# Up projection of an encoder layer: the transposes of six column groups moved from TensorE to DMA, on 16-bit planes that ScalarE splits and joins

## The chip, the cores and the metric

The kernel runs on one core of a Trainium2 chip. The metric is the device time of one launch in microseconds. Three runs of the kernel before gave 1339.71 to 1340.78 us, with a median of 1339.76 us.

## The reference

One layer of a transformer trunk on 256 tokens of width 2048, in float32: two kinds of attention, gates, an output projection, and then the part that is touched here, an MLP with a squared ReLU.

```python
h = rms_norm(x, norm_mlp_pre[l])                                             # 256 x 2048
u = jnp.square(jax.nn.relu(jnp.einsum('bsd,df->bsf', h, w_up[l])))           # 256 x 8192
x = x + rms_norm(jnp.einsum('bsf,fd->bsd', u, w_down[l]), norm_mlp_post[l])  # 256 x 2048
```

The up projection leaves `u` with tokens on the 128 partitions. The down projection sums over the 8192 columns of `u`, so it needs `u` transposed: columns on the partitions, tokens along the row.

## The kernel before

Each float32 operand of a product is split into a high part (`h`, rounded to TensorE's float32r) and a low part (`l`, what the rounding left). A product is then three matmuls: high by high, high by low, low by high. For each weight block ScalarE makes the high part (`CAST u_4h<-u_4r`) and VectorE subtracts to get the low one (`TENSOR_TENSOR u_4l<-u_4r,u_4h`). Every low part therefore waits for a cast of ScalarE.

The up projection runs in eight groups `g` of 1024 columns. A group is eight steps, each with one weight block of 256 by 1024 numbers (`u_0r` to `u_7r`, 1 MB, issued on SyncE's queue). Where a step is marked "seven" in `UPS`, the product is done with seven multiplications instead of eight, on sums of quarters of the weight block: `u_0t`, `u_3t`, `u_5t` are these sums, made by VectorE, `eh` their high parts (ScalarE), `el` their low ones (VectorE). Two tiles of sums stand after one another, the second made from the first, so VectorE and ScalarE take turns on them. The list `UPS` sets the order of the blocks within a group: 1, 2, 0, 4, 3, 6, 5, 7. Weights are prepared two steps ahead of their use (`Weights.next`), in a pool `wp` of three buffers each for the raw block, its high and its low part. A shared pool `pages` of 27 buffers holds everything else.

At the end of a group ScalarE and VectorE take the eight accumulators out of PSUM (`combine` and `u_piece`), scale and rectify them, and leave two tiles `z[0]`, `z[1]` of 128 tokens by 1024 columns. While the next group runs, `up_each(n)`, called ahead of each step `n` of it, treats these tiles: at steps 1 and 2 `u_T` transposes 512 columns each on TensorE (eight matmuls with the identity into two PSUM banks) and ScalarE squares them on the way out; at steps 3 and 5 `u_sets` splits the transposed `u` again into high and low parts (`ah`, `al`, for one of the two halves with the sums `sm`, made by VectorE). GpSimd's queue stores these parts to memory (`keeph`, `keepl`), and the down projection loads them again much later. The last group's results and those of the one before it are needed at once, and their transposes stand in other places (group 7 and the first steps of the down projection).

A scheduler orders the instructions of each engine: it plays the program with costs of its own and puts first what it finds ready first. Semaphores for all dependences are added after that. Each engine works through its row in that order; an instruction that waits holds up all that stand behind it on its engine, and a DMA issued from ScalarE's queue stands in ScalarE's row.

Of the kernel before, what the change touches and what calls it, by code (L numbers as in the profile page):

```python
# [10 lines left out]

F32 = mybir.dt.float32
F32R = mybir.dt.float32r
AF = mybir.ActivationFunctionType
ALU = mybir.AluOpType
AX = mybir.AxisListType

P = 128
D = 2048
T = 256  # L20
KD = D // P
DFF = 4 * D
# [28 lines left out]
def encoder_layer(ctx: ExitStack, tc: tile.TileContext, a, out):  # L51
    nc = tc.nc
# [12 lines left out]
    def page(shape, dt, name):  # L65
        return pages.tile(shape, dt, tag="pg", name=name)
# [4 lines left out]
    def t2k(name, dt=F32):  # L71
        return tmp.tile([P, 2, T], dt, tag="t2k", name=name, bufs=7)
# [6 lines left out]
    def small(w, name):  # L79
        return tiny.tile([P, w], F32, tag=f"s{w}", name=name)  # L80
# [37 lines left out]
    def split(raw, name, pieces=2, after=(), then=None):  # L118
# [3 lines left out]
        _, nk, cw = (P, len(raw), 512) if listed else raw.shape  # L122
        hi = wp.tile([P, nk, cw], F32R, tag="hi", name=f"{name}_h")
        lo = wp.tile([P, nk, cw], F32R, tag="lo", name=f"{name}_l")
        prev = front if then else ()
# [170 lines left out]

    hT = [page([P, 2, 512], F32R, f"hT{i}") for i in range(8)]

    def x_part(k):
# [3 lines left out]
        g = g_pre[:, k : k + 1]  # L303
        i = nc.scalar.activation(d[:, :T], src, AF.Copy, scale=g).ins
        j = nc.vector.scalar_tensor_tensor(  # L305
# [30 lines left out]
    def x_squares(i):  # L336
        for t in range(2):
            j = junk512("jx0").rearrange("p a b -> p (a b)")
            nc.scalar.activation(
                j, xp[i][:, t], AF.Square, accum_out=ssx[:, t * 4 + i : t * 4 + i + 1]  # L340
            )
# [10 lines left out]
    def head_constants():  # L352
# [5 lines left out]
        le = small(2, "le")  # L358
        nc.scalar.activation(le, ls, AF.Exp)
        nc.vector.scalar_tensor_tensor(  # L360
# [55 lines left out]
    def parts(dst, at, src):  # L416
        hi, lo = dst
        nc.scalar.copy(hi[at], src)
        nc.vector.tensor_sub(lo[at], src, hi[at].bitcast(F32))
# [34 lines left out]
    def v_evac(dst):  # L454
        hi, lo = dst

        def evac(t, ps):
            r = rx[:, t : t + 1]
            nc.scalar.activation(hi[:, t], ps, AF.Copy, scale=r)
            nc.vector.scalar_tensor_tensor(  # L460
# [5 lines left out]
    def p_transposed(p, name):  # L466

        pt = bank(f"{name}_pt")
        for kt in range(2):
            for t in range(2):  # L470
# [4 lines left out]
                )  # L475
        r = [t2k(f"{name}_pT{i}", F32R) for i in range(2)]
        parts(r, slice(None), pt.rearrange("p (k q) -> p k q", k=2))
        return r

    def diff_head(h, qT, kT, v, hl, sc):  # L480
        p = t2k(f"dp{h}")
        for t in range(2):
# [19 lines left out]
            for c in range(2):  # L502
                nc.scalar.activation(
                    e[:, c],
                    s[:, c * T : (c + 1) * T],
                    AF.Exp,
                    bias=nbs[:, c : c + 1],
# [27 lines left out]
        for t in range(2):  # L535
            nc.scalar.activation(
                on[:, t], o[:, t * T : (t + 1) * T], AF.Square, accum_out=ss[:, t : t + 1]
            )
# [5 lines left out]
        for eb in range(2):  # L544
            for t in range(2):
# [4 lines left out]
                )  # L550
        ot = page([P, 2, 512], F32R, f"oaT{h}")
        for eb in range(2):
# [8 lines left out]
    def na_head(h, qT, kT, v, hl):  # L561
# [47 lines left out]
        if h % 2 == 0:  # L609
            oT["nt", h // 2] = page([P, 2, 512], F32R, f"onT{h}")  # L610
        ot = oT["nt", h // 2][:, h % 2]
# [283 lines left out]
    for h in range(2):  # L895
        gate = []
        for br, gc, src, o in (("a", GA, a["w_branch_a"], "a"), ("b", GB, a["w_branch_b"], "n")):
            z = [page([P, 2, 512], F32, f"g{br}{h}{t}") for t in range(2)]
# [183 lines left out]
    def first_up(n):  # L1082
        for t, c in {2: [(1, 1), (0, 2)], 3: [(1, 2), (0, 3)], 4: [(1, 3)]}.get(n, ()):
            residual_parts(t, c)
        if n == 5:
            for t in range(2):
                mlp_squares(t)
                mlp_scale(t)
            for i in range(4):
                kd = dram.tile([P, 1024], F32, name=f"keepx{i}", tag=f"keepx{i}")  # L1090
                nc.gpsimd.dma_start(kd, x2[i])
                kept["x", i] = kd
# [67 lines left out]
    def u_T(cg, z):  # L1160
# [12 lines left out]
            )  # L1173
        return u

    def u_sets(cg, u):

        got = act_sets(cg, u)
        if NG - 4 <= cg < NG - 2:
            sets[0, cg] = got  # L1180
# [34 lines left out]
                uw.ask(wd[:, :, cg, j, g * 1024 : (g + 1) * 1024], f"d{g}{cg}{j}", seven, page)  # L1215
    uz = None
    us = {}
    for g in range(DFF // 1024):
        z = Late(lambda g=g: [page([P, 2, 512], F32, f"u{g}{t}") for t in range(2)])

        def up_each(n, g=g, uz=uz):
            if not g:
                first_up(n)
                if n == 7:
                    for i in (0, 3, 5):
                        f = page([P, 2, T], F32, f"h2f{i}")
                        for k in range(2):
                            d = hT2[i][:, k].bitcast(F32)
                            nc.vector.tensor_add(f[:, k], d[:, :T], d[:, T:])
                        h2sum[i] = sums_of(f[:, 0], f[:, 1], f"h2s{i}")  # L1230
                return
            cg = g * 2 - 3 + n
            if n in (1, 2):
                us[cg] = u_T(cg, uz)
            steps = (3, 5) if g < DFF // 1024 - 1 else (1, 2)
            if n in steps:
                cg = g * 2 - 2 + steps.index(n)
                u_sets(cg, us[cg])

        wide_group(  # L1240
            f"u{g}",
            ups(g),
            uw,
            h2stat7,
            h2stat8,
            (1, 2, 3, 7),
            z,
            partial(u_piece, z=z),
            each=up_each,
            turn=None if g else turn_rows,  # L1250
            after={} if g else {2: scaled[0]},
        )
        uz = z
# [102 lines left out]
    for g in range(2):  # L1356
        pr = Products(f"p{g}", (1, 2, 3, 7))
        pr.in_order = True
        for bi, b in enumerate(blocks[g]):
            end = bi == len(blocks[g]) - 1  # L1360
            for n, (cg, j, seven) in enumerate(down_steps(g, bi)):
# [42 lines left out]
                for which in range(4):  # L1404
# [4 lines left out]
                    if last:  # L1409
                        bank_, t, half = PLAIN[which]  # L1410
# [65 lines left out]
```

## Time and profile before

| | before |
|---|---|
| median of three runs | 1339.76 us |
| the profiled execution | 1339.83 us |
| its span, first to last instruction | 1338.1 us |
| mean granted TensorE clock | 0.997 |
| TensorE matmul busy | 1326.8 us (99%) |
| VectorE busy | 1097.9 us (82%) |
| ScalarE busy | 739.4 us (55%) |
| transposes `uT` on TensorE | 128, of which 32 are those of group 7 and of the start of the down projection |

The profiled execution is 0.07 us above the median. The 1.7 us between its time and its span are start and end. In rows of the time line the columns are start, duration, engine, line, operation, output and inputs with shapes, count, and in brackets how long the engine had been idle before it and on what. In the chain, the columns are start, duration, engine, tile, line, count. The busy time of an engine is a sum over its instructions, and weight loads of TensorE (PEld) lie beside its matmuls.

### The profile page before, as it was taken

How to read it: one execution, taken by the hardware profiler on the slowest of the kernel's cores; microseconds unless marked ns; L12 is line 12 of the kernel's file. 1: busy time of each engine (PE TensorE's matmuls, PEld its weight loads, DVE VectorE, ACT ScalarE, POOL GpSimd, SP SyncE). 2: the span in 40 equal slices, each digit the busy share in tenths (PEclk: the TensorE clock that was granted, in tenths of full speed). 3: DMA queues.
4: the chain of work that ended last, by engine and by line, in shares of the span. 5: the costliest groups of instructions: out<-in, count | busy, mean ns of one | idle time of the engine just before them, and what ended most of it. 6: DMA issues, size and time to landing. Idle time of an engine off the chain costs nothing.

```text
span 1338.1 us, 16265 instructions
## 1 busy us (share of the span) xinstructions
PE 1326.8 (99%) x6297; PEld 1112.1 (83%) x6297; DVE 1097.9 (82%) x1279; ACT 739.4 (55%) x866; POOL 38.5 (3%) x71
## 2 busy tenths in 40 slices
PE   9999999999999999999999999999999999999997
PEld 8888888888888888888888888888888888888885
DVE  7978866667777888885688999999978888898886
ACT  6655554544545555555476666666555554555542
POOL 0000000000000000000100000000000000000000
PEclk9999999999999999999999999999999999999998
DMA  9874655564565656567657777877797998798995
GB/s 343 279 219 162 197 168 176 184 186 157 189 220 172 207 187 213 184 233 256 228 184 274 243 251 270 302 238 245 251 362 287 402 375 314 265 376 331 353 356 202
DMA packets 113981, 335.85 MB, mean 251 GB/s; under 512 B 16752, under 2 KB 17008, under 8 KB 113904
## 3 DMA queue, kind: packets, MB, share of 16 engines
q1 hardware_dynamic: 94512, 266.13, 57.9%
q10 hardware_dynamic: 12672, 43.00, 8.4%
q0 software_dynamic: 6720, 25.69, 5.0%
q8 instruction: 49, 0.80, 0.2%
q14 instruction: 28, 0.23, 0.0%
HBM read 307.01 MB, written 29.61 MB: 252 GB/s over the span
## 4 chain that ended last, share of the span: by engine, by line
PE 96%; DMA 1%; DVE 1%; ACT 0%; SPq 0%; issue 0%; DVEq 0%; POOLq 0%; POOL 0%; ACTq 0%
PE u L740 25%; PE p L740 24%; PE ga L740 6%; PE gb L740 6%; PE ba L740 3%; PE bb L740 3%; PE y L740 3%; PE qn_p L221 2%; PE kn_p L221 2%; PE ka_p L221 2%; PE qn_p L223 1%; PE kn_p L223 1%; PE qa_p L221 1%; PE vn_p L264 1%; PE va_p L265 1%; PE vn_p L265 1%
## 5 line engine op out<-in xcount | busy, mean ns | idle before, releaser
L221 PE MATMUL qn_p<-hT,qn_h 128*128 128x512 f32 x128 | 45.8, 399 | 0.0
L221 PE MATMUL ka_p<-hT,ka_h 128*128 128x512 f32 x128 | 45.1, 397 | 0.2 <-DVE rope_s L291 0.2
L221 PE MATMUL kn_p<-hT,kn_h 128*128 128x512 f32 x128 | 45.3, 397 | 0.0
L221 PE MATMUL qa_p<-hT,qa_h 128*128 128x512 f32 x128 | 43.9, 402 | 0.4 <-DVE hT L305 0.4
L740 PE MATMUL u<-u_2h,h2T 128*128 128x512 f32 x128 | 44.0, 396 | 0.0
L740 PE MATMUL u<-u_1h,h2T 128*128 128x512 f32 x128 | 43.4, 390 | 0.0
L740 PE MATMUL u<-u_4h,h2T 128*128 128x512 f32 x128 | 43.2, 391 | 0.0
L740 PE MATMUL u<-u_7h,h2T 128*128 128x512 f32 x128 | 41.0, 389 | 0.0
L740 PE MATMUL u<-u_6h,h2T 128*128 128x512 f32 x128 | 41.0, 389 | 0.0
L223 PE MATMUL qn_p<-hT,qn_l 128*128 128x256 f32 x128 | 35.9, 281 | 0.0
L223 PE MATMUL kn_p<-hT,kn_l 128*128 128x256 f32 x128 | 35.7, 280 | 0.0
L223 PE MATMUL ka_p<-hT,ka_l 128*128 128x256 f32 x128 | 35.1, 280 | 0.0
L223 PE MATMUL qa_p<-hT,qa_l 128*128 128x256 f32 x128 | 32.4, 281 | 0.0
L145 DVE TENSOR_TENSOR y_l<-y_w,y_h 128x1024 fp32r<-128x1024 f32 x16 | 19.0, 1221 | 11.9 <-ACT y_h L137 11.9
L221 PEld LDWEIGHTS ka_p<-hT,ka_h 128*128 128x128 f32 x128 | 23.8, 188 | 5.7 <-DVE rope_s L291 0.7
L221 PEld LDWEIGHTS qn_p<-hT,qn_h 128*128 128x128 f32 x128 | 24.1, 188 | 5.2
L145 DVE TENSOR_TENSOR kn_l<-kn_w,kn_h 128x1024 fp32r<-128x1024 f32 x16 | 19.0, 1220 | 11.3 <-ACT kn_h L137 11.2
L221 PEld LDWEIGHTS kn_p<-hT,kn_h 128*128 128x128 f32 x128 | 23.9, 188 | 5.2
L221 PEld LDWEIGHTS qa_p<-hT,qa_h 128*128 128x128 f32 x128 | 23.9, 191 | 5.2 <-ACT qa_h L143 0.6
L740 PEld LDWEIGHTS u<-u_1h,h2T 128*128 128x128 f32 x128 | 24.0, 188 | 5.0
L740 PEld LDWEIGHTS u<-u_6h,h2T 128*128 128x128 f32 x128 | 24.0, 188 | 5.0
L740 PEld LDWEIGHTS u<-u_7h,h2T 128*128 128x128 f32 x128 | 24.0, 188 | 5.0
(1622 smaller groups left out, 4556.9 us busy)
## 6 DMA issues: line engine op xcount, KB each, us to landing
bh<-keeph ACTq DMA_DIRECT2D x30, 512.0 KB, 8.9
bl<-keepl ACTq DMA_DIRECT2D x30, 512.0 KB, 10.8
keeph<-ah POOLq DMA_DIRECT2D x18, 512.0 KB, 3.6
keepl<-al POOLq DMA_DIRECT2D x18, 512.0 KB, 7.0
va_w<-in_w_in SPq DMA_DIRECT2D x8, 1024.0 KB, 5.3
qn_w<-in_w_in SPq DMA_DIRECT2D x8, 1024.0 KB, 5.3
kn_w<-in_w_in SPq DMA_DIRECT2D x8, 1024.0 KB, 5.2
vn_w<-in_w_in SPq DMA_DIRECT2D x8, 1024.0 KB, 5.1
```

The costliest lines, as they stand in the source:

```text
L145: sub = nc.vector.tensor_sub(lo[part], src, hi[part].bitcast(F32)).ins
L221: nc.tensor.matmul(ps[b], hi[:, k % 4, cs], mv, start=(k == 0), stop=False)
L223: nc.tensor.matmul(ps[b][:, :T], lo[:, k % 4, cs], mv[:, :T], start=False, stop=(k == nk - 1))
L264: nc.tensor.matmul(ps[t], sh, hi[:, k % 4], start=(k == 0), stop=False)
L265: nc.tensor.matmul(ps[t], sh, lo[:, k % 4], start=False, stop=False)
L740: ins = nc.tensor.matmul(self.ps[i], st, mv[:, blk], start=i not in self.begun, stop=last and n == 2).ins
```

## The change

In groups 1 to 6 the transposes leave TensorE. At step 0 `u_halves` copies each result tile into planes of 16 bits on ScalarE: the low halves of all words side by side, then the high halves (`us`). A DMA on ScalarE's queue transposes a plane of 128 partitions by 1024 values into the tile `uh` (`DMA_TRANSPOSE`); there are four of them in a group. At steps 3 and 5 `u_joined` interleaves the two transposed planes into words again on ScalarE (`COPY u<-uh`, 2048 values of 16 bits for each partition) and then squares them in place (`ACTIVATE u<-u`, 1024 values). The splits behind that (`u_sets`) stay as they were. Group 7 and the start of the down projection keep the transposes on TensorE.

```diff
+    def u_halves(z, g):
+        got = [page([P, 2, 4, T], U16, f"uh{g}{c}") for c in range(2)]
+        for t in range(2):
+            zp = page([P, 2, 2, 512], U16, f"us{g}{t}")
+            for c in range(2):
+                words = z[t][:, c].bitcast(U16).rearrange("p (c h) -> p h c", h=2)
+                nc.scalar.copy(zp[:, c], words)
+                nc.scalar.dma_start(
+                    got[c].rearrange("p h k q -> p (h k) q")[:, :, t * P : (t + 1) * P],
+                    zp[:, c].rearrange("p h c -> p (h c)"),
+                    transpose=True,
+                )
+        return got
+
+    def u_joined(cg, halves_):
+        u = page([P, 4, T], F32, f"u{cg}")
+        words = u.rearrange("p k q -> p (k q)").bitcast(U16).rearrange("p (c h) -> p h c", h=2)
+        nc.scalar.copy(words, halves_.rearrange("p h k q -> p h (k q)"))
+        nc.scalar.activation(u, u, AF.Square)
+        return u
...
             cg = g * 2 - 3 + n
-            if n in (1, 2):
+            moved = g < DFF // 1024 - 1
+            if moved and n == 0:
+                uh[g] = u_halves(uz, g)
+            if not moved and n in (1, 2):
                 us[cg] = u_T(cg, uz)
-            steps = (3, 5) if g < DFF // 1024 - 1 else (1, 2)
+            steps = (3, 5) if moved else (1, 2)
             if n in steps:
                 cg = g * 2 - 2 + steps.index(n)
-                u_sets(cg, us[cg])
+                u_sets(cg, u_joined(cg, uh[g][steps.index(n)]) if moved else us[cg])
```

The scheduler orders all rows anew. The lines of the changed file are numbered one higher up to the new functions and 24 or more higher behind them. In the rows below, `u4_3h` is the high part of block 3 in group 4, `u4_3t0` and `u4_3t1` its two tiles of sums, `u4_3eh0` and `u4_3el0` the high and low part of the first; `u6` and `u7` are the two halves of the transposed result of group 3, and `ah6...`, `al7...` their parts.

The first place is the first half of group 4. On ScalarE, from the second tile of sums of block 0 to the cast of block 5, before:

```order
L693 CAST u4_0eh1_6988<-u4_0t1_6978 128x1024
L675 CAST u4_4h_7022<-u4_4r_7020 128x2048
L1171 ACTIVATE u6_7026<-uT60_7027 128x512
L1171 ACTIVATE u6_7026<-uT61_7033 128x512
L693 CAST u4_3eh0_7074<-u4_3t0_7067 128x1024
L680 CAST u4_3h_7065<-u4_3r_7063 128x1536
L675 CAST u4_6h_7122<-u4_6r_7120 128x2048
L693 CAST u4_3eh1_7078<-u4_3t1_7068 128x1024
```

and after:

```order
L694 CAST u4_0eh1_6964<-u4_0t1_6954 128x1024
L1184 COPY us40_6970<-u30_6904 128x1024 x2
L676 CAST u4_4h_7010<-u4_4r_7008 128x2048
L1185 DMA_TRANSPOSE uh40_6968<-us40_6970 128x8x128
L1185 DMA_TRANSPOSE uh41_6969<-us40_6970 128x8x128
L1184 COPY us41_6975<-u31_6905 128x1024 x2
L681 CAST u4_3h_7040<-u4_3r_7038 128x1536
L676 CAST u4_6h_7084<-u4_6r_7082 128x2048
L1185 DMA_TRANSPOSE uh40_6968<-us41_6975 128x8x128
L1185 DMA_TRANSPOSE uh41_6969<-us41_6975 128x8x128
L694 CAST u4_3eh0_7049<-u4_3t0_7042 128x1024
L694 CAST u4_3eh1_7053<-u4_3t1_7043 128x1024
```

Two copies now stand ahead of the cast of block 4, two DMA issues and two more copies between it and the cast of block 3, and two DMA issues ahead of the casts of the sums of block 3. Behind the last row follow `u4_5h`, the joining copy of `u6`, and `u4_7h`.

At the same place VectorE's row was before:

```order
L694 TENSOR_TENSOR u4_0el1_6989<-u4_0t1_6978,u4_0eh1_6988 128x1024
L681 TENSOR_TENSOR u4_3t0_7067<-u4_3r_7063 128x1024
L677 TENSOR_TENSOR u4_4l_7023<-u4_4r_7020,u4_4h_7022 128x2048
L682 TENSOR_TENSOR u4_3t1_7068<-u4_3t0_7067,u4_3r_7063 128x512
L694 TENSOR_TENSOR u4_3el0_7075<-u4_3t0_7067,u4_3eh0_7074 128x1024
L684 TENSOR_TENSOR u4_3l_7066<-u4_3r_7063,u4_3h_7065 128x1536
```

and is after:

```order
L695 TENSOR_TENSOR u4_0el1_6965<-u4_0t1_6954,u4_0eh1_6964 128x1024
L678 TENSOR_TENSOR u4_4l_7011<-u4_4r_7008,u4_4h_7010 128x2048
L682 TENSOR_TENSOR u4_3t0_7042<-u4_3r_7038 128x1024
L685 TENSOR_TENSOR u4_3l_7041<-u4_3r_7038,u4_3h_7040 128x1536
L683 TENSOR_TENSOR u4_3t1_7043<-u4_3t0_7042,u4_3r_7038 128x512
L678 TENSOR_TENSOR u4_6l_7085<-u4_6r_7082,u4_6h_7084 128x2048
L684 TENSOR_TENSOR u4_3t1_7043<-u4_3t1_7043,u4_3r_7038 128x512
L695 TENSOR_TENSOR u4_3el0_7050<-u4_3t0_7042,u4_3eh0_7049 128x1024
L695 TENSOR_TENSOR u4_3el1_7054<-u4_3t1_7043,u4_3eh1_7053 128x1024
L685 TENSOR_TENSOR u4_5l_7141<-u4_5r_7138,u4_5h_7140 128x1536
L678 TENSOR_TENSOR u4_7l_7181<-u4_7r_7178,u4_7h_7180 128x2048
```

The sum `u4_3t0`, which needs no cast, stood ahead of `u4_4l` and now stands behind it, and `u4_3l` has moved ahead of the sums of its block.

The second place is the end of the group, where the second half `u7` is split. ScalarE before:

```order
L693 CAST u4_5eh0_7184<-u4_5t0_7177 128x1024
L693 CAST u4_5eh1_7188<-u4_5t1_7178 128x1024
L675 CAST u5_1h_7253<-u5_1r_7251 128x2048
L1126 CAST ah70_7219<-u7_7082 128x1024
L675 CAST u5_2h_7287<-u5_2r_7285 128x2048
L767 COPY u40_7278<-u40_7101 128x512
```

and after:

```order
L694 CAST u4_5eh0_7149<-u4_5t0_7142 128x1024
L694 CAST u4_5eh1_7153<-u4_5t1_7143 128x1024
L1196 COPY u7_7184<-uh41_6969 128x2x1024
L1197 ACTIVATE u7_7184<-u7_7184 128x1024
L1127 CAST ah70_7187<-u7_7184 128x1024
L768 COPY u40_7246<-u40_7063 128x512
```

The casts of the next group's blocks 1 and 2 have moved up ahead of this place, and the joining copy and the square have come in ahead of `ah70`. VectorE at this place, before:

```order
L683 TENSOR_TENSOR u4_5t1_7178<-u4_5t1_7178,u4_5r_7173 128x512
L694 TENSOR_TENSOR u4_5el0_7185<-u4_5t0_7177,u4_5eh0_7184 128x1024
L694 TENSOR_TENSOR u4_5el1_7189<-u4_5t1_7178,u4_5eh1_7188 128x1024
L677 TENSOR_TENSOR u5_1l_7254<-u5_1r_7251,u5_1h_7253 128x2048
L1127 TENSOR_TENSOR al70_7220<-u7_7082,ah70_7219 128x1024
L677 TENSOR_TENSOR u5_2l_7288<-u5_2r_7285,u5_2h_7287 128x2048
```

and after:

```order
L678 TENSOR_TENSOR u5_2l_7256<-u5_2r_7253,u5_2h_7255 128x2048
L683 TENSOR_TENSOR u4_5t1_7143<-u4_5t0_7142,u4_5r_7138 128x512
L695 TENSOR_TENSOR u4_5el0_7150<-u4_5t0_7142,u4_5eh0_7149 128x1024
L684 TENSOR_TENSOR u4_5t1_7143<-u4_5t1_7143,u4_5r_7138 128x512
L695 TENSOR_TENSOR u4_5el1_7154<-u4_5t1_7143,u4_5eh1_7153 128x1024
L1128 TENSOR_TENSOR al70_7188<-u7_7184,ah70_7187 128x1024
```

Between `u4_5el1` and `al70` a subtraction of block 1 stood before; now nothing stands between them, and the first step of `combine` (`u40`, `u45`) comes right behind `al70`.

More of the change, by code (lines that the diff above doesn't have):

```diff
@@ L13 @@
 F32R = mybir.dt.float32r
+U16 = mybir.dt.uint16
 AF = mybir.ActivationFunctionType
@@ L1217, in encoder_layer @@
     us = {}
+    uh = {}
     for g in range(DFF // 1024):
```

## Prediction

> **What bounds the kernel now.** I read the page's first part, then the chain that ended last, then one group of the up projection by stretch, by waits and by time line.
>
> ```profile
> span 1338.1 us, 16265 instructions
> PE 1326.8 (99%) x6297; PEld 1112.1 (83%) x6297; DVE 1097.9 (82%) x1279; ACT 739.4 (55%) x866; POOL 38.5 (3%) x71
> ```
>
> TensorE is busy for the whole span. The chain says the same of the groups that are changed. Here is one of them, with the first row of the next:
>
> ```profile
> 789.19 0.87 PE uT L1168 x8
> 790.06 2.74 PE u L740 x12
> 792.80 0.87 PE uT L1168 x8
> 793.68 38.78 PE u L740 x171
> 832.46 0.87 PE uT L1168 x8
> ```
>
> A group lasts 832.46 - 789.19 = 43.27 us, and there is nothing in it but matmuls and the sixteen transposes, 2 x 0.87 = 1.74 us of it, 0.109 us for each. What the other engines do in about the same stretch is in the next row; its columns are length, busy time and count of TensorE, its weight loads, VectorE, ScalarE and GpSimd, then clock, DMA share and GB/s.
>
> ```profile
> 793.30:836.60 43.30, 43.30 (x202) 36.04 (x201) 40.02 (x40) 27.44 (x28) 3.23 (x6) 1.00 0.75 261
> ```
>
> So TensorE is the bound, but VectorE has only 3.3 us to spare. ScalarE has 15.9 us. What each waited for in that stretch:
>
> ```profile
> DVE u_0el L694 <- ACT u_0eh L693: 1.1, 1, 1.1
> DVE u_1l L677 <- ACT u_1h L675: 0.9, 1, 0.9
> DVE u_6l L677 <- ACT u_6h L675: 0.7, 1, 0.7
> DVE u_7l L677 <- ACT u_7h L675: 0.4, 1, 0.4
> ...
> ACT u_0h L680 <- PE u L740: 5.1, 1, 5.1
> ACT u_5eh L693 <- DVE u_5t L681: 3.7, 1, 3.7
> ACT u_0eh L693 <- DVE u_0t L683: 2.6, 1, 2.6
> ```
>
> All of VectorE's waits are for casts of ScalarE. ScalarE's idle time lies in a few places, in front of things that were not ready. It is no store on which work put elsewhere can draw. A reader should keep this: two engines that hand work to each other in a fixed order can both have time to spare and yet stop each other.
>
> **The transposes that go.** 6 groups x 16 x 0.109 = 10.4 us leave TensorE, and a group would take 43.27 - 1.74 = 41.53 us if TensorE stayed the bound. Whether it does depends on VectorE: its 40.02 us of work leave 1.5 us of idle time for a group.
>
> **What ScalarE gets.** In each of the six groups: four copies of 1024 16-bit values, two joining copies of 2048, two squares of 1024, four DMA issues. It loses four squares of 512 out of PSUM. The trace has no 16-bit copy; the nearest rows are the casts with as many values:
>
> ```profile
> 832.54 1.91 ACT L675 CAST u_4h<-u_4r 128x2048 fp32r<-128x2048 f32 x1
> 834.35 1.08 ACT L1171 ACTIVATE u<-uT 128x512 f32<-128x512 f32 x2
> 835.31 1.06 ACT L693 CAST u_3eh<-u_3t 128x1024 fp32r<-128x1024 f32 x1
> 836.26 1.48 ACT L680 CAST u_3h<-u_3r 128x1536 fp32r<-128x1536 f32 x1
> ```
>
> From start to start that is 1.81 us for 2048 values, 0.95 for 1024, 0.54 for 512, and 1.39 for 1536 with the same overlap of 0.09. So 4 x 0.95 + 2 x 1.81 + 2 x 0.95 - 4 x 0.54 = 7.2 us more in a group, 34.6 in all. I take the 16-bit copies at these prices and keep half and double of them for the range.
>
> The price of a transpose's issue, h, during which ScalarE's row stands still, is not in the trace. ScalarE's queue has plain DMA issues, and a row for stores tells how long a transfer of 512 KB is under way:
>
> ```profile
> L1143 ACTq DMA_DIRECT2D bh<-keeph x42: 326/442/1506, 984.0 to 1295.9; - x42
> ...
> keeph<-ah POOLq DMA_DIRECT2D x18, 512.0 KB, 3.6
> ```
>
> The lower bound is the median of such an issue, 0.44 us. The upper is 3.6 us, as if the queue were held until a transfer had landed. I take 1.5 us, the longest issue in the row: a transpose writes 1024 pieces of 256 bytes, so it is nearer to the hard cases than to the usual one. With that, ScalarE has 34.6 + 6.0 = 40.6 us of work in a group. By totals it would fit into 41.53.
>
> **Where VectorE stops.** It doesn't fit by order. I walk through the new rows of ScalarE and VectorE shown with the change. VectorE's prices:
>
> ```profile
> 832.46 1.23 DVE L694 TENSOR_TENSOR u_0el<-u_0t,u_0eh 128x1024 fp32r<-128x1024 f32 x1 [1.11 <-ACT u_0eh L693]
> 833.60 1.22 DVE L681 TENSOR_TENSOR u_3t<-u_3r 128x1024 f32<-128x1024 f32 x1
> 834.73 2.29 DVE L677 TENSOR_TENSOR u_4l<-u_4r,u_4h 128x2048 fp32r<-128x2048 f32 x1
> 836.93 0.68 DVE L682 TENSOR_TENSOR u_3t<-u_3t,u_3r 128x512 f32<-128x512 f32 x1
> 837.54 1.22 DVE L694 TENSOR_TENSOR u_3el<-u_3t,u_3eh 128x1024 fp32r<-128x1024 f32 x1
> 838.67 1.75 DVE L684 TENSOR_TENSOR u_3l<-u_3r,u_3h 128x1536 fp32r<-128x1536 f32 x1
> ```
>
> Start to start: 2.20 us for 2048 values, 1.67 for 1536, 1.13 for 1024, 0.61 for 512. Let the clock be 0 where ScalarE starts `u4_0eh1`; VectorE takes a result 0.03 us after its end.
>
> - `u4_4l`: ScalarE casts until 0.95, does two copies until 2.85, and `u4_4h` ends at 4.76. VectorE is through with `u4_0el1` at 2.21 and has nothing else ahead in its row: idle 2.6 us. Before, it had `u_3t` to do there, and the cast came at once.
> - `u4_3l`: behind `u4_4h` come two issues (2h) and two copies; `u4_3h` ends at 8.04 + 2h. VectorE is through with `u4_4l` and `u4_3t0` at 8.12: idle 2h - 0.05, that is 2.95.
> - `u4_3el0`: `u4_6h`, two more issues, and the cast ends at 10.81 + 4h = 16.81. VectorE, after `u4_3l`, two small sums and `u4_6l`, is there at 16.16: idle 0.7.
> - `u4_7l`: `u4_5h` ends at 19.14, then the joining copy, and `u4_7h` ends at 22.77. VectorE, through with `u4_5l` at 20.84, is idle for 1.95.
> - `u4_5el1`: the second sum is now made behind `u4_5el0`, so the cast and VectorE take turns, as in block 0, where the trace shows 1.1 us of idle time: 1.1.
> - `al70`: behind `u4_5eh1` come the joining copy, the square, which has to wait for its end, and the cast, 3.95 us and 0.03 for each hand-over; VectorE has 1.13 us of work for that time: idle 2.8.
>
> The wait for `u_0el`, 1.1 us, stays; those for `u_1l`, `u_6l` and `u_7l` are replaced. The sum is 1.1 + 2.6 + 2.95 + 0.7 + 1.95 + 1.1 + 2.8 = 13.2 us, and a group lasts 40.0 + 13.2 = 53.2 us, against 43.27. The 10.4 us that TensorE saves are then worth nothing: it waits for low parts.
>
> VectorE may first use up its lead over TensorE, once:
>
> ```profile
> 812.31 2.48 DVE L694 TENSOR_TENSOR u_5el<-u_5t,u_5eh 128x1024 fp32r<-128x1024 f32 x2
> 818.46 0.39 PE L740 MATMUL u<-u_5el,h2s 128*128 128x512 f32 x1
> ```
>
> The first of the two ends at about 813.5, 4.9 us ahead of its use. Sum: 6 x (53.2 - 43.27) - 4.9 = 55 us.
>
> **The rest of the change.** The DMA queues: the transposes move 1 MB for a group beside 11.3 MB (261 GB/s x 43.3 us), in more time, so weight loads get no denser; free. SyncE issues a load when its buffer is read; it is late with VectorE, not the cause. GpSimd's stores run later with `ah` and `al` and are not needed before the down projection. PSUM banks of `uT` come free: nothing waited for them. The down projection keeps its work and nearly its order: nothing.
>
> Whether the transposes have landed in time: the third one of a group is issued at 9.76 + 2h = 12.8, and its joining copy is due at 13.05 + 4h = 19.05, so 6.3 us are covered. Rows of ScalarE's loads:
>
> ```profile
> bh<-keeph ACTq DMA_DIRECT2D x12, 384.0 KB, 4.7
> ...
> DMA to landing us min/median/max: 3.6/7.8/14.8
> ```
>
> 256 KB are nearest to the first row, so I count nothing; at 7.8 us it would be 1.5 us more in a group, at 14.8 8.5.
>
> The Trainium skill, "VectorE: DVE Perf Modes", in its section on the three transpose paths, has 1309 ns for a 128 by 128 transpose through DMA against 390 on TensorE, and its rules take TensorE where the result may go to PSUM: a rule against this change, and the trace's 0.109 us on TensorE makes the case stronger. "DMA: Bandwidth & Descriptors", section on latency, gives transposes 261 GB/s, an estimate of 1.0 us for 256 KB; by that figure the landing is covered and the sum stays.
>
> **Sum.** The profiled execution took 1339.83 us, 0.07 above the median: 1339.8 + 55 = 1395 us.
>
> **Rivals.**
> - The totals decide. ScalarE runs ahead of VectorE in its spare time, TensorE stays the bound, and the 10.4 us come out: 1329.4 us. For it speak 40.0 and 40.6 us of work in 41.5; against it the walk. It would have to find less than 1.5 us of idle time in a group, or 2.3 with the lead spread over six groups (4.9 / 6 = 0.8), where I count 13.2. Between the two, with about 3.3 + 0.8 us of idle time, lies no change.
> - The transposes land late, and ScalarE stands in front of the joining copy with the casts of block 7 and the next group behind it. From 6.3 us on each us costs 6 in all: 1404 us at 7.8, 1446 at 14.8. Loads share the DMA engines, 75% busy, which speaks for it; the small size speaks against.
> - The transposes themselves are slow and go one after another, so that four fill most of a group. If one took the 8.9 us that a load of 512 KB took to land (below), the third would land 26.7 us after the first's issue at 4.66, against 19.05: 12.3 us more in a group, 1395 + 74 = 1469 us. The Trainium skill's 1309 ns for a block ("VectorE: DVE Perf Modes", the section named above), times eight blocks, would make 10.5 us for each; by the same steps that is an estimate of 1498 us.
>
> ```profile
> bh<-keeph ACTq DMA_DIRECT2D x30, 512.0 KB, 8.9
> ```
>
> **How the numbers follow.** The walk as above has 0.70, late landing 0.20, slow transposes 0.04, the totals 0.04, no change 0.02. About 0.2% (2.7 us) is what can be told from no change. So faster 0.04, same 0.02, slower 0.94. The walk's own ends: with h = 0.44 the idle times are 1.1 + 2.6 + 0.8 + 0 + 0.6 + 1.1 + 2.8 = 9.0, a group of 49.0, and 1370 us; with h = 3.6, four h for a group, 1395 + 6 x 4 x 2.1 = 1445 us. 16-bit copies at half price take 3.7 us from a group (0.95 at two places, 0.9 at two): 1373; at double price they add 7.4: 1439. The range from 1370 to 1445 holds the walk and most of late landing.
>
> **What the profile would show.** Right: groups 2 to 6 last 51 to 56 us in the chain, which passes through VectorE and ScalarE; VectorE's waits for `u_4h`, `u_3h`, `u_7h` and `ah` are new, 2 to 3 us each time; TensorE waits for `u_5el`. The issues on ScalarE's queue last about 1.5 us. Wrong: a wait of ScalarE for `uh` (landing), groups of 41.5 us (the totals), or issues and 16-bit copies of quite another length.

## The result and the profile after

The changed kernel takes 1394.49 us (median of four runs, 1393.9 to 1395.32) against 1340.27 us before: a ratio of 1.0406, 95% interval 1.0394 to 1.0419. That is 54.2 us slower; 1395 was forecast.

The first rows of the page:

```profile
span 1392.7 us, 16121 instructions
PE 1342.3 (96%) x6201; PEld 1111.5 (80%) x6201; DVE 1100.1 (79%) x1279; ACT 793.0 (57%) x890; POOL 38.5 (3%) x71
```

Three stretches of 53 us, one group each (columns as in the row by stretch of before):

```profile
740.00:793.00 53.00, 47.02 (x183) 36.70 (x183) 39.37 (x39) 35.66 (x32) 2.95 (x6) 0.90 0.75 243
793.00:846.00 53.00, 46.52 (x183) 36.17 (x183) 39.98 (x40) 36.43 (x32) 3.10 (x6) 0.90 0.73 231
846.00:899.00 53.00, 45.65 (x183) 35.74 (x183) 40.78 (x41) 36.43 (x32) 3.38 (x7) 0.94 0.74 236
```

VectorE has as much to do as before, 40 us, but now in 53 us instead of 43.3. ScalarE has 8 to 9 us more than the 27.4 of before and is still idle for 17. TensorE does fewer things, and each takes longer: the granted clock is down to 0.90 to 0.94 here, where it stood at 1.00.

VectorE's rows with idle time ahead of them, in one group, from the time line of after (start, duration, engine, line, operation; in brackets the idle time and whom it waited for):

```profile
845.35 1.23 DVE L1128 TENSOR_TENSOR al<-u,ah 128x1024 fp32r<-128x1024 f32 x1 [3.35 <-ACT ah L1127]
857.74 1.23 DVE L695 TENSOR_TENSOR u_0el<-u_0t,u_0eh 128x1024 fp32r<-128x1024 f32 x1 [1.12 <-ACT u_0eh L694]
861.44 2.29 DVE L678 TENSOR_TENSOR u_4l<-u_4r,u_4h 128x2048 fp32r<-128x2048 f32 x1 [2.48 <-ACT u_4h L676]
865.14 1.76 DVE L685 TENSOR_TENSOR u_3l<-u_3r,u_3h 128x1536 fp32r<-128x1536 f32 x1 [0.27 <-ACT u_3h L681]
877.00 2.29 DVE L678 TENSOR_TENSOR u_7l<-u_7r,u_7h 128x2048 fp32r<-128x2048 f32 x1 [2.44 <-ACT u_7h L676]
881.88 2.29 DVE L678 TENSOR_TENSOR u_1l<-u_1r,u_1h 128x2048 fp32r<-128x2048 f32 x1 [0.18 <-ACT u_1h L676]
887.52 2.29 DVE L678 TENSOR_TENSOR u_2l<-u_2r,u_2h 128x2048 fp32r<-128x2048 f32 x1 [1.08 <-ACT u_2h L676]
893.26 1.23 DVE L695 TENSOR_TENSOR u_5el<-u_5t,u_5eh 128x1024 fp32r<-128x1024 f32 x1 [1.11 <-ACT u_5eh L694]
897.82 1.23 DVE L1128 TENSOR_TENSOR al<-u,ah 128x1024 fp32r<-128x1024 f32 x1 [3.33 <-ACT ah L1127]
```

From `al` to `al` a group lasts 897.82 - 845.35 = 52.5 us (the shortest of the five such groups; the longest takes 53.7), and the idle times in it (the eight behind the first) are 12.0 us. Every one of them is a wait for ScalarE, and the long ones stand where a splitting or a joining copy comes ahead of the cast. TensorE stands behind that, as its own waits in the up projection show (whole time, times, longest):

```profile
PE u L741 <- DVE u_5el L695: 12.7, 6, 2.4
PE u L741 <- ACT u_5eh L694: 12.0, 7, 2.7
```

The transposes and the joining copies (durations are least, median and longest; the last row is the time from issue to landing):

```profile
L1185 ACTq DMA_TRANSPOSE uh<-us x24: 1247/1361/3612, 702.6 to 969.6; - x24
L1196 ACT COPY u<-uh x12: 2480/2510/2536, 714.1 to 998.6; 128x2048 uint16<-128x2048 uint16 x12
...
DMA to landing us min/median/max: 3.1/5.1/7.8
```

Nobody waits for `uh`: the landing is covered. An issue lasts 1.36 us at the median and 3.61 at the longest. What it holds up, the total does not tell, and the experiments had to.

### The profile page after: what moved, and what is told of

The parts are those of the page before. It is cut to its first block, busy times and chain, and to the rows that moved or that the text cites. A ratio compares the mean times of both kernels' runs of the same rounds, so it can differ in the third digit from the quotient of the medians.

```text
span 1392.7 us, 16121 instructions
## 1 busy us (share of the span) xinstructions
PE 1342.3 (96%) x6201; PEld 1111.5 (80%) x6201; DVE 1100.1 (79%) x1279; ACT 793.0 (57%) x890; POOL 38.5 (3%) x71
## 5 line engine op out<-in xcount | busy, mean ns | idle before, releaser
L741 PE MATMUL u<-u_1h,h2T 128*128 128x512 f32 x128 | 47.3, 422 | 5.9 <-DVE u L1209 5.9
L741 PE MATMUL u<-u_2h,h2T 128*128 128x512 f32 x128 | 44.2, 400 | 0.0
L741 PEld LDWEIGHTS u<-u_1h,h2T 128*128 128x128 f32 x128 | 25.8, 201 | 13.2 <-DVE u L1209 7.6
L678 DVE TENSOR_TENSOR u_4l<-u_4r,u_4h 128x2048 fp32r<-128x2048 f32 x8 | 18.3, 2293 | 21.4 <-ACT u_4h L676 21.4
L1128 DVE TENSOR_TENSOR al<-u,ah 128x256 fp32r<-128x256 f32 (+2 forms) x26 | 18.7, 749 | 19.0 <-ACT ah L1127 19.0
L1210 ACT ACTIVATE u<-u,r 128x512 f32<-128x512 f32 x32 | 21.4, 712 | 18.0 <-DVE u L1209 13.4
L1196 ACT COPY u<-uh 128x2048 uint16<-128x2048 uint16 x12 | 30.1, 2509 | 0.0
L678 DVE TENSOR_TENSOR u_7l<-u_7r,u_7h 128x2048 fp32r<-128x2048 f32 x8 | 18.3, 2292 | 14.7 <-ACT u_7h L676 14.7
L741 PEld LDWEIGHTS u<-u_2h,h2T 128*128 128x128 f32 x128 | 25.3, 197 | 5.6
L741 PE MATMUL u<-u_5eh,h2s 128*128 128x512 f32 x36 | 17.5, 537 | 12.0 <-ACT u_5eh L694 12.0
```

Of the source, the lines that this page charges most:

```text
L678: nc.vector.tensor_sub(l1, raw, h1.bitcast(F32))
L741: ins = nc.tensor.matmul(self.ps[i], st, mv[:, blk], start=i not in self.begun, stop=last and n == 2).ins
L1128: nc.vector.tensor_sub(lo[:, at], src, hi[:, at].bitcast(F32))
L1196: nc.scalar.copy(words, halves_.rearrange("p h k q -> p h (k q)"))
L1210: nc.scalar.activation(zt, zt if summed else ps, AF.Relu, scale=r2[:, t : t + 1])
```

## The experiments

Twelve kernels ran, each timed beside the kernel before. The theories: A, the added copies cost their length; B, the issues hold ScalarE; C, the order that the scheduler writes around the new instructions is the cost; D, a copy costs only at a place where VectorE is next in line for what stands behind it.

| kernel | what it is | us | ratio to before (95%) |
|---|---|---|---|
| pe_only | TensorE's transposes left out, nothing added | 1342.26 | 1.0016 (1.0007 to 1.0026) |
| order_before | before, ScalarE's row chained | 1340.64 | 1.0005 (0.9996 to 1.0014) |
| before_act | before, with the change's copies added | 1364.57 | 1.0182 (1.0167 to 1.0198) |
| no_dma | after, without the DMA transposes | 1365.59 | 1.0189 (1.0170 to 1.0208) |
| sp | after, transposes from SyncE's queue | 1377.51 | 1.0280 (1.0265 to 1.0296) |
| dma_twice | after, each transpose issued twice | 1446.67 | 1.0833 (1.0771 to 1.0894) |
| order_act | after, ScalarE's row chained | 1386.64 | 1.0344 (1.0329 to 1.0360) |
| order_sp | the same, from SyncE's queue | 1368.70 | 1.0208 (1.0193 to 1.0223) |
| late_joins | as order_sp, copies at other steps | 1349.54 | 1.0069 (1.0052 to 1.0086) |
| half | half of the transposes moved | 1338.56 | 0.9991 (0.9981 to 1.0000) |
| pool_joins | as order_sp, joins on GpSimd | 1374.38 | 1.0259 (1.0245 to 1.0273) |
| half_pool | half moved, copies on GpSimd | 1358.10 | 1.0126 (1.0108 to 1.0145) |

### What the removed transposes were worth

```diff
 # pe_only, against the kernel before
         for b in range(2):
+            if moved:
+                to = u[:, b * 2 : b * 2 + 2]
+                nc.scalar.activation(to.rearrange("p k q -> p (k q)"), z[b][:, cg % 2], AF.Square)
+                continue
             pt = bank(f"uT{cg}{b}")
```

> The kernel before without the 96 transposes of the six groups: the four squares of 512 are made straight from the results, so ScalarE and VectorE do the same amount as before and TensorE 10.4 us less (the output is then not the layer's, since nothing is transposed). The gain of the change with no price at all. If TensorE's time comes through: 1330. If VectorE, which has 3.3 us to spare in a group of 43.3, already stops it at its waits: 1333 to 1338.

Measured: 1342.26 us, 2.5 us above the kernel before, timed beside it (1339.79). 10.4 us of TensorE's work are gone, and nothing comes out. This was outside all that was expected. The chain of waits of one group shows what stands in the way:

```profile
803.30 1.93 ACT u_7h L675
805.25 2.30 DVE u_7l L677
807.57 8.99 DMA u_2r<-in_w_up
816.66 1.92 ACT u_2h L675
818.60 1.23 DVE u_2l L677
...
820.81 1.22 DVE al L1127
```

A load can be issued only when VectorE has read the raw block that held its buffer; the block of `u_7` is free at 807.6, the load of `u_2` lands 9 us later, and the sums with which the group ends stand behind `u_2l` in VectorE's row. A group here takes 44.0 us (`u_4l` at 791.50 and at 835.48), TensorE working for 42.1 of them. The gain was not there to be had in this order of the work. But the order is not that of the kernel before: with the transposes gone, the scheduler put `ah` and `al` of the second half behind `u_2h` and `u_2l`, where they had stood ahead of them, so VectorE's 1.1 us for `al` no longer fill its wait for `u_2h` (1.76 us in this group). What the removal would bring in the old order, no run shows.

### The copies alone

In before_act `more` makes the four splitting copies of `u_halves` and `joined` the joining copy of `u_joined`, both into spare pages.

```diff
 # before_act, against the kernel before
+            if moved and n == 0:
+                uh[g] = more(uz, g)
             if n in (1, 2):
                 us[cg] = u_T(cg, uz)
...
+                if moved:
+                    joined(cg, uh[g][steps.index(n)])
                 u_sets(cg, us[cg])

 # no_dma, against the changed kernel
-                nc.scalar.copy(zp[:, c], words)
-                nc.scalar.dma_start(..., transpose=True)
+                nc.scalar.copy(got[c][:, :, :, t * P : (t + 1) * P], words)
```

> The kernel before with its TensorE transposes kept, and in the six groups the change's copies added as work whose result nobody reads: four splitting copies of 1024 at the first step, a joining copy of 2048 ahead of each of the two casts of ah. No DMA transposes. That is 4 x 0.95 + 2 x 2.45 = 8.7 us more ScalarE work in a group. Theory A (the extra copies stand ahead of casts that VectorE waits for): 30 to 55 us slower than before, 1370 to 1395. Theory B (the transposes' issues): the copies fit into ScalarE's 15.9 us of idle time, 1340 to 1350. Theory C (order): here the scheduler puts the sums u_3t ahead of u_4l in some groups, and the copies stand after u_4h in others; 1345 to 1365.

> The 24 transposes are left out: the splitting copies write their values straight into the pages that the joining copies read, so ScalarE does as many copies of the same lengths (the output is then not the layer's, since nothing is transposed). The scheduler, which no longer has the issues in ScalarE's row, also puts some instructions back: VectorE's first sum u_3t stands ahead of u_4l again, as before the change. Theory A (ScalarE's extra copies are the cost, the transposes themselves cost nothing): 1385 to 1400 us. Theory B (the issues hold ScalarE, 2.95 + 0.7 us of idle time for a group as the prediction had it): 6 x 3.65 = 22 us less than the changed kernel, about 1372. Theory C (the order in which ScalarE's and VectorE's rows are written is the cost): most of the 54 us goes, 1340 to 1365.

Measured: 1364.57 and 1365.59 us, 24.3 and 25.3 us above the kernel before. The two agree, with TensorE's transposes and without, though the scheduler orders their rows differently (in four of before_act's groups the splitting copies stand ahead of `u_4h`, in two behind it); the copies cost 24 to 25 us of the 54 as the scheduler places them. That is less than A said of both and more than B's 1340 to 1350 for before_act; C's ranges end at 1365, between the two. The other 29 us belong to the transposes and to what they do to the rows. The added copies last what they last in the change (1.04 us, and 2.53 to 2.54 against 2.51).

### The issues

```diff
 # sp
-                nc.scalar.dma_start(
+                nc.sync.dma_start(

 # dma_twice
+                for to in (got, more):
-                nc.scalar.dma_start(got[c]...
+                    nc.scalar.dma_start(to[c]...
```

> The same transposes, issued from SyncE's queue instead of ScalarE's; all copies as in the changed kernel. The scheduler's order changes with it in the same direction as when the transposes are left out (u_3t ahead of u_4l). Theory A: 1385 to 1400 us. Theory B (issues hold ScalarE): about 1372. Theory C (order): 1340 to 1365, and no more than 5 us from the run without transposes, as landing was covered.

> Every transpose is issued twice from ScalarE's queue, the second time into a spare page that nobody reads; the copies are unchanged. Theory B: the issues (1.36 us each in the changed kernel's trace) hold ScalarE, so 24 more of them cost another 22 to 33 us: 1417 to 1428. Theories A and C: within 8 us of the changed kernel, 1388 to 1402. If the transfers' traffic is what delays the loads of w_up (the cast u_2h waits up to 2.8 us for u_2r in a group), twice the traffic makes that wait longer: 6 x 2.8 = 17 us more, 1411.

Measured: 1377.51 us from SyncE's queue, 17.0 us less than from ScalarE's, and 1446.67 us with every transpose doubled, 52.2 us more (the four runs of this kernel spread from 1436.58 to 1462.24). For sp, B's 1372 is nearest; A and C missed, C also with its 5 us from no_dma, which are 11.9. None of the theories had said 1446 for dma_twice. The waits of ScalarE in the up projection of dma_twice (whole time, times, longest):

```profile
ACT us L1185 <- issue: 32.0, 6, 7.0
ACT u_3eh L694 <- issue: 29.6, 6, 6.4
...
ACT u_2h L676 <- DMA u_2r<-in_w_up: 8.8, 5, 4.8
```

Four issues in a row hold the next instruction for 3.2 to 7.0 us, twice in a group, 61.6 us in all; the wait for `u_2r`, 8.8 us in all, is no longer than the 11.0 us of the changed kernel, so the traffic is not seen to do it. The issues do hold ScalarE. In the changed kernel, though, the same view has hardly any such wait:

```profile
ACT u_2h L676 <- DMA u_2r<-in_w_up: 11.0, 6, 2.8
...
ACT u_3eh L694 <- issue: 1.7, 1, 1.7
ACT us L1184 <- issue: 1.1, 1, 1.1
```

To tell the issue from the order, the next two kernels fix the order of ScalarE's row in groups 1 to 6: each instruction is chained behind the one written before it (`act_row` takes the place of `nc.scalar` in the up projection; in their profiles these rows have the helper's line, L675).

```diff
+        def __getattr__(self, op):
+            def run(*args, **kw):
+                if "on" not in row_end:
+                    return getattr(self.engine, op)(*args, **kw)
+                end = row_end.get(self.name)
+                with tc.issue_after(end) if end else nullcontext():
+                    got = getattr(self.engine, op)(*args, **kw)
+                row_end[self.name] = got.ins
+                return got
+            return run
```

> The changed kernel, transposes still issued from ScalarE's queue, with one thing added: in the six groups the scheduler may no longer choose the order of ScalarE's row; each instruction there is chained behind the one written before it (first sums u_3t then stand ahead of u_4l on VectorE, u_3eh ahead of u_6h and u_5eh ahead of u_1h and u_2h on ScalarE). Work is the same. Theory C (of the 54 us, the 30 that the added copies do not explain are the written order): 1360 to 1372 us. Theory B (the issues on ScalarE's queue hold it; four in a row held it for 5 to 7 us where every transpose was issued twice): the chain changes nothing in that, 1380 to 1400, and above the run from SyncE's queue by 12 us or more.

> The same with the transposes issued from SyncE's queue; ScalarE's and VectorE's rows are then the same, instruction for instruction, as in the run with the chained row and ScalarE's queue, so that the difference is what the issues on ScalarE's queue cost by themselves. Theory C: within 5 us of that run. Theory B: 12 to 20 us less than it.

> The kernel before with nothing changed but the chain along ScalarE's row in the six groups. It shows what the chain is worth by itself. Theory D and C: within 3 us of the kernel before, since TensorE bounds it and stays busy. If the chain itself explained the better times of the chained kernels: 1330 to 1336.

Measured: 1386.64 from ScalarE's queue, 1368.70 from SyncE's, 17.9 us between them with the same rows on ScalarE and VectorE. The chain alone does nothing to the kernel before (1340.64). This decides for B on this question: issued on ScalarE's queue, the 24 transposes cost 18 us more than on SyncE's. The time line of ScalarE's row in order_act shows where (ACTq is the queue that issues):

```profile
851.22 1.99 ACT L675 COPY us<-u 128x1024 uint16<-128x1024 uint16 x2
852.29 4.53 ACTq L1205 DMA_TRANSPOSE uh<-us  x2
856.87 2.00 ACT L675 COPY us<-u 128x1024 uint16<-128x1024 uint16 x2 [3.65 <-issue]
857.95 1.74 ACTq L1205 DMA_TRANSPOSE uh<-us  x1
858.77 1.91 ACT L675 CAST u_4h<-u_4r 128x2048 fp32r<-128x2048 f32 x1
859.72 1.33 ACTq L1205 DMA_TRANSPOSE uh<-us  x1
861.15 1.49 ACT L675 CAST u_3h<-u_3r 128x1536 fp32r<-128x1536 f32 x1 [0.47 <-ACT u_4h L675]
```

The first pair of issues stands between two pairs of copies. An issue can start only when its copy has ended, and what stands behind it can't start before the issue is through: ScalarE is idle for 3.65 us. Most of that is one issue: of the 4.53 us the second takes 3.24. In five of the six groups it takes 3.0 to 3.4 us here, and 3.0 to 3.4 from SyncE's queue in order_sp too, where it holds nothing of ScalarE's; what makes it so much longer than the median of 1.36, no run shows. The second pair has the cast of `u_4` ahead of it in the row, which runs meanwhile, and 0.47 us remain. In its view of waits, the six idle times of the first kind make 20.1 us, which stand against the 17.9; order_sp has no such row:

```profile
ACT us L675 <- issue: 20.1, 6, 3.8
```

In the changed kernel the scheduler, left free, put a cast ahead of both pairs:

```profile
857.61 1.99 ACT L1184 COPY us<-u 128x1024 uint16<-128x1024 uint16 x2
858.68 1.25 ACTq L1185 DMA_TRANSPOSE uh<-us  x1
859.51 1.90 ACT L676 CAST u_4h<-u_4r 128x2048 fp32r<-128x2048 f32 x1
860.02 1.66 ACTq L1185 DMA_TRANSPOSE uh<-us  x1
861.73 1.99 ACT L1184 COPY us<-u 128x1024 uint16<-128x1024 uint16 x2 [0.32 <-ACT u_4h L676]
```

So the hold itself is 0.32 us there, where the second issue lasts 1.66 us and runs beside the cast. Yet taking the issues away from that queue still brings 17.0 us (sp), and the scheduler then writes another order: `u_3t` ahead of `u_4l` on VectorE again, and `u_3eh` ahead of `u_6h` on ScalarE, each in three of the six groups. That the price of an issue is paid as idle time in one order and through the order itself in the other is how I read the two pairs; shown is the sum, 17 to 18 us each time. C's strong form, that a repaired order would bring the changed kernel to 1372 or less, has failed.

The Trainium skill, "DMA: Bandwidth & Descriptors", section "Issuing engines are not separate DMA queues", says that issuing from several engines saves only the sequencer's time for the issue, "usually small relative to the DMA itself". The first half agrees with the 17.9 us; as to the second, 1.36 us stand here against 5.1 us to landing, and the small part is the one that cost.

### Amount or place

Steps from 8 on stand for the next group: 13 and 15 are its steps 5 and 7, counted from 0.

```diff
 # late_joins, against order_sp
-            if moved and n == 0:
+            if cs and n == 2:
                 uh[g] = u_halves(uz, g, cs)
...
+                joins = {0: 13, 1: 15}

 # half: one half of the columns, from SyncE's queue, row chained
+            cs = () if last else (1,)
+            if cs and n == 0:
...
+                joins = {1: 7}
```

> The same amount of work on every engine as in the changed kernel, transposes from SyncE's queue, ScalarE's row chained, but at other places: the splitting copies at the third step of a group (behind u_3eh) instead of the first, and each joining copy with its square and its casts of ah at the sixth and eighth step of the next group, so that nothing waits for them. Theory A (the 24 us that the added copies cost are their amount, 8.5 us for a group): 1362 or more. Theory D (they cost where VectorE is next in line for the cast behind them, and little where ScalarE has time): 1336 to 1350.

> Only the odd half of each group's results goes by DMA (two splitting copies of 1024, one joining copy at the eighth step, 12 transposes from SyncE's queue), the even half by TensorE as before; ScalarE's row chained. TensorE saves half, 6 x 8 x 0.109 = 5.2 us, and ScalarE gets half, 4.3 us a group. Theory A (amount): half of 24 less what TensorE saves, 1347 to 1353. Theory D (place): 1335 to 1342.

Measured: 1349.54 us with all of the change's work on every engine, 19.2 us less than order_sp. What was changed is only the steps at which the copies stand, and with the joins the squares and splits behind them; VectorE's row, which is not chained, the scheduler then ordered anew (`u_4l` ahead of two of the three sums `u_3t` in most groups, behind all three in order_sp). With half of the work it is 1338.56 us. A is out, D holds, here at the upper end of its range: 8.8 us of added ScalarE work in a group cost 28.4 us at one place and 9.2 at another. In late_joins some waits for the stored parts appear at the start of the down projection, 4.2 us for `bh` and 1.5 for `bl`, as the stores come a group later. Most of the 9.2 us lies there: from its first matmul to its last, the up projection takes 350.0 us (349.9 before), and from there to the last matmul of the down projection 339.2 us pass (331.1 before). So the up projection lost at these steps about what it gained from TensorE, at most 10.4 us.

In half, TensorE bounds the kernel again, as the chain over two of its groups shows:

```profile
by line: PE u L761 98.4%; PE uT L1189 1.8%; issue 0.1%
...
788.80 0.65 PE uT L1189 x6
...
831.46 0.66 PE uT L1189 x6
```

A group takes 831.46 - 788.80 = 42.66 us, 0.61 less than before, where 0.87 us of transposes went. In the traces the up projection is 3.9 us shorter than before (346.0 against 349.9), and the down projection 1.0 us longer. Over all, 1.7 us of 1340 are gained, with an interval that ends at 1.0000: no difference that this measurement can tell. It is the best version that ran; none was shown to beat the kernel before.

### The copies on GpSimd

```diff
 # pool_joins
-        act_row.copy(words, halves_.rearrange("p h k q -> p h (k q)"))
+        nc.gpsimd.tensor_copy(words, halves_.rearrange("p h k q -> p h (k q)"))
```

half_pool moves the other half of the columns than half, at other steps (splitting copies at step 2, joining copies at step 5), and makes both kinds of copy on GpSimd.

> All transposes by DMA from SyncE's queue, the splitting copies on ScalarE and ScalarE's row chained as in the run at 1368.7 us, at the same steps; only the twelve joining copies are made by GpSimd, which takes 2 x 2.5 us a group from ScalarE. Theory A (what stands in ScalarE's row ahead of the casts costs its length): 6 x 2 to 3 us less, 1350 to 1357; the casts of ah still wait for the join. Rival (GpSimd's copy takes over 5 us, so that the squares and casts behind it come later than with ScalarE's 2.5): 1365 to 1385.

> Only the even half of each group's results goes by DMA (12 transposes from SyncE's queue); its splitting copies (third step) and joining copies (sixth step) are made by GpSimd, which is busy for 38.5 us of the span, so ScalarE gets no added copy and VectorE nothing. ScalarE's row is chained. TensorE saves 6 x 8 x 0.109 = 5.2 us. Theory D (a copy costs only where VectorE is next in line for what stands behind it): the 5.2 us come through, 1334 to 1337. Rival (GpSimd's copies of 16-bit values are slow, or disturb VectorE): 1340 or more.

Measured: 1374.38 us, 5.7 above order_sp, although ScalarE is rid of 31 us; and 1358.10 us (three runs of 1355.86 to 1358.31, and one of 4759 us, of which there is no trace and whose cause is open). Both are the rival's numbers, but not for the rival's first reason: GpSimd's copy takes 2.79 us, hardly more than ScalarE's 2.53. The reason is on VectorE. From the time lines of pool_joins, GpSimd first, then VectorE:

```profile
772.02 2.69 POOL L1216 COPY u<-uh 128x2048 uint16<-128x2048 uint16 x1
```

```profile
772.25 4.03 DVE L705 TENSOR_TENSOR u_5l<-u_5r,u_5h 128x1536 fp32r<-128x1536 f32 x1
```

The subtraction takes 1.75 us in order_sp. Here it ends 1.57 us after GpSimd's copy has ended (776.28 against 774.71), so hardly any of its 1.75 us of work can have been done before. Summed over the kernel, from the pages of order_sp and of pool_joins:

```profile
PE 1331.3 (97%) x6201; PEld 1111.8 (81%) x6201; DVE 1099.8 (80%) x1279; ACT 792.4 (58%) x890; POOL 38.5 (3%) x71
```

```profile
PE 1332.6 (97%) x6201; PEld 1106.5 (81%) x6201; DVE 1126.3 (82%) x1279; ACT 761.2 (55%) x878; POOL 74.8 (5%) x83
```

Twelve copies lengthen VectorE's work by 26.5 us, 2.2 us each: they moved from ScalarE to VectorE. Beside this, ScalarE's squares wait 8.3 us in all for GpSimd's copies. In half_pool the transposes also take longer to land, 7.0 to 9.7 us instead of 3.8 to 5.8 in half. The Trainium skill, "SBUF — State Buffer", section "Who interferes with whom", has this as a lock: a VectorE instruction with two inputs in SBUF and a GpSimd instruction that reads SBUF exclude each other, and the later one waits for the whole of the earlier. The trace agrees, with the two rows above.

## Why the prediction was right, point by point

- **TensorE's 10.4 us are worth nothing.** Right for the change: TensorE waits for low parts there, as the prediction said (12.7 us for `u_5el` in all). Without any price they bring nothing either (pe_only), but for another reason than the prediction's: there a load waits for a buffer, in rows that the scheduler had ordered anew. In another order they do count: half gains 0.61 of 0.87 us in a group.
- **ScalarE's added work, 7.2 us a group.** The splitting copies last 1.04 us as the casts they were priced by. The joining copy was mis-sized: from start to start it takes 2.37 us (872.68 to 875.05 in the group shown; its length is 2.51), against the 1.81 of a cast of 2048 values. ScalarE has 36.4 us in a group, where 34.6 had been counted.
- **The issue, h = 1.5 us.** The length was right, 1.36. The step that failed, in a prediction that came out, is what it holds: idle times of 2.95 us at `u_3l` and 0.7 at `u_3el0` were counted from issues that start only behind `u_4h`; the issues start as soon as their copies end, beside `u_4h`, and 0.27 and 0 us were measured. The holding exists, 3.65 us for a pair, in another order (order_act).
- **The waits.** `u_0el` 1.12 (1.1 predicted), `u_4l` 2.48 (2.6), `u_7l` 2.44 (1.95), `u_5el1` 1.11 (1.1), `al70` 3.33 (2.8): right in place and nearly in size; the last has the longer joining copy ahead of it. `u_1l`, 0.18, and `u_2l`, 1.08, were not foreseen: ScalarE's cast `u_2h` stands and waits for the load of `u_2r`, which is issued when VectorE, itself late, has left a buffer.
- **The sum.** 12.0 us of idle time where 13.2 were counted, 52.5 us for a group against 53.2, and the total within 0.5 us of 1394.49. That it came so near is luck, since errors of both signs cancelled; the total is better than its parts: 3.65 - 0.27 = 3.4 us too much for the issues and 0.1 at `u_4l`, against 2.3 too little in four other places (0.5, 0.5, 0.2, 1.1) and half a microsecond more of busy time on VectorE. Between the first and the sixth `al` of the sums five groups last 989.46 - 725.62 = 263.8 us, 52.8 each, against 938.38 - 718.78 = 219.6 before: 44.2 us; 6.8 come ahead of the first, and 3 behind the sixth. At 52.8 us, six groups of the prediction's form, 6 x (52.8 - 43.27), would make 57 us, so 3 us were saved where a lead of 4.9 was counted; these rows do not show that it was the lead, as the first of the five groups took 46.5 us, and not 43.27, before the change too.

```profile
725.62 1.23 DVE L1128 TENSOR_TENSOR al<-sm,ah 128x1024 fp32r<-128x1024 f32 x1 [0.19 <-ACT ah L1127]
...
989.46 1.22 DVE L1128 TENSOR_TENSOR al<-sm,ah 128x1024 fp32r<-128x1024 f32 x1
```

```profile
718.78 1.22 DVE L1127 TENSOR_TENSOR al<-sm,ah 128x1024 fp32r<-128x1024 f32 x1
...
938.38 1.22 DVE L1127 TENSOR_TENSOR al<-sm,ah 128x1024 fp32r<-128x1024 f32 x1
```

- **Landing, DMA traffic, the down projection at nothing.** Right: no wait for `uh`, 5.1 us to landing where up to 6.3 were covered (the prediction's two estimates for one transpose, 1.0 and 10.5 us, both missed); `u_2r` lands in 6.1 us (median) before and after; and from the last matmul of the up projection to the last of the down projection it is 331.0 us, where it was 331.1. Only the wait for `u_2r` was not nothing: SyncE issues that load late, as foreseen, but ScalarE then stands for it, 11.0 us in all, and so, in the group shown, does VectorE for the 1.08 us at `u_2l`.
- **The rivals.** Totals did not decide: late_joins has the same totals as the change and is 45 us faster, 9.2 above the kernel before. Late landing and slow transposes did not come.

Of the 54.2 us, then, 25.3 are there without any transpose (no_dma), 11.9 more with the transposes on SyncE's queue (sp), and 17.0 more with them on ScalarE's. The 11.9 are not taken apart: with ScalarE's row chained the same transposes stand 3.1 us above no_dma, so most of them may be order too, but the rows of those two kernels differ in other ways.

## What to carry to other kernels

Where two engines hand work to each other in a fixed order, price an added instruction by who is next in line behind it, not by the idle total of its engine: the same copies cost 28 us at one step and 9 at another. A DMA issued from a compute engine's queue right behind the instruction that feeds it holds what follows for the whole issue, unless a long instruction that needs nothing stands between the two; an idle queue like SyncE's is the better place. And before paying for a removal, leave the thing out and time it: the 10.4 us that the change takes from TensorE bring nothing even for free in the order that the scheduler then writes. Compare the rows of such a run with those of before, though, for a removal also changes the order.

## What the hardware showed that was not expected

- A transpose of 128 by 1024 16-bit values takes 1.25 to 1.66 us to issue from ScalarE's queue in the group shown, against 0.44 for a plain transfer (median, in the kernel before), and lands in 3.1 to 7.8 us. Issues of one queue come one after another, and single ones take far longer than the median: the second of the pair in order_act takes 3.24 us, and the longest from ScalarE's queue in the changed kernel 3.61. Why, no run shows.
- A copy that interleaves two planes of 16 bits takes ScalarE 2.51 us for 2048 values, against 1.91 for a cast of 2048 words.
- A VectorE subtraction with two inputs in SBUF that started 0.23 us behind a GpSimd copy took 4.03 us instead of 1.75, and ended 1.57 us after the copy.
- In five groups of the changed kernel, with TensorE busy for 83 to 89% of the time, the granted TensorE clock is 0.90 to 0.96; it is 1.00 in the group of before, where TensorE is busy throughout, and in that of pe_only (96%). 183 matmuls take 45.7 to 47.3 us of busy time at 0.90 to 0.94, where pe_only's 185 take 42.1. The busy share alone does not decide it: pool_joins has a stretch of 50 us with TensorE busy for 87% and a clock of 1.00.
